# Where split weights lie in on-chip memory: one fixed byte offset for all feature-major projections instead of a different one per call

## The chip, the cores and the metric

The kernel runs on one core of one Trainium2 chip. The metric is the device time of one launch in microseconds (us). Before the change the median of three runs is 2135.49 us (2133.76 to 2135.58). The profile shown below is of one further execution, which took 2132.74 us; from its first to its last instruction it spans 2131.0 us. The engines are named as in the profile: PE is the matrix engine (its instruction that streams the moving operand), PEld its weight load, ACT the scalar engine, DVE the vector engine, POOL the general engine, SP the queue that issues the DMAs.

## The reference

One layer of a hybrid encoder on 256 tokens of width 2048, all in float32:

```python
h = rms_norm(x, norm_mix_g)
x = x + hybrid_mixer(h, ...)          # w_in: 2048 -> 18464, retention + gated DeltaNet, w_out: 2048 -> 2048
h = rms_norm(x, norm_x_g);  mem_n = rms_norm(mem, norm_mem_g)
x = x + cross_attention(h, mem_n, w_xq, w_xkv, w_xo)      # 4 heads, 256 memory tokens
h = rms_norm(x, norm_ffn_g)
x = x + square(relu(h @ w_ff1)) @ w_ff2                   # 2048 -> 8192 -> 2048
return rms_norm(x, norm_final_g)
```

Nearly all of the arithmetic is dense projections of 256 tokens through weights that are read from the chip's main memory once.

## The kernel before, in words

**Products in two parts.** Each float32 operand is kept as two float32r operands, a high part and a low part, with value = high + low. A product takes three of the four partial products: high x high, high x low, low x high. The activations lie as `q` tiles: 128 partitions by 4 feature blocks by 512 columns, of which the first 256 are the high parts of the 256 tokens and the other 256 the low parts (`quad.both` is all 512).

**Fetching weights.** `fetch` (lines 75 to 97) brings one piece of 1 MB into a tile `raw` (one of three buffers), with one DMA on the SP queue. It then makes two halves of 1024 columns each: ACT copies the half into a tile `whi` (line 94, which rounds to float32r), DVE subtracts that from `raw` into a tile `wlo` (line 95). `whi` and `wlo` have three buffers each. Each buffer is 1024 + 64 floats long per partition, 4352 bytes, and the 1024 floats that are used start `a` floats into it; the argument `at` gives `a` for `whi` and for `wlo`.

**Two kinds of projection.** Both go through `fetch`.

- `chunk` (lines 122 to 152) is token-major: the stationary operand is 128 tokens of `q`, the moving operand is 512 columns of `whi` or `wlo` (lines 135 to 137). It takes four fetches a call and uses the default `at=(0, 0)`.
- `blocks` (lines 159 to 187) is feature-major: the stationary operand is a block of 128 x 128 from `whi` or `wlo`, the moving operand is `q`. For each block and each of the 16 feature blocks it issues a pair: line 177 multiplies the block of `whi` with all 512 columns of `q`, line 178 the block of `wlo` with the 256 high columns. A call with `nb=2` has 16 x 2 = 32 pairs, takes two fetches (four halves of 8 pairs), and gives 256 output features. At its end ACT and DVE add the two halves of the PSUM tile (lines 182 and 183) and hand the result on.

**The placement in `blocks`.** A counter `turn` counts the calls of `blocks` in the order of the program. Call n, counted from 0, takes `ah, al = divmod(29 * n % 64, 8)`, and `at=(8 * ah, 8 * al)` floats: the used part of `whi` starts 32 * ah bytes, that of `wlo` 32 * al bytes into its buffer, with ah and al from 0 to 7. As 29 is odd, 64 calls in a row go through all 64 pairs (ah, al), and call n + 64 has the pair of call n again. Such a pair is called a placement below.

**The order of the calls of `blocks`**, 97 in all:

| calls | what | when, us |
|---|---|---|
| 0 | decay inputs, `nb=1`, 16 pairs | 86 |
| 1 to 8 | keys of the cross-attention | 114 to 212 |
| 9 to 40 | q, k, v of the DeltaNet (6 a group) and q, k of the retention (2 a group), four groups | 212 to 992 |
| 41 to 48 | `w_out` | 1117 to 1208 |
| 49 to 56 | queries of the cross-attention | 1208 to 1316 |
| 57 to 64 | `w_xo` | 1317 to 1412 |
| 65 to 96 | first MLP matrix, four groups of 8 | 1412 to 2035 |

In the MLP each group of 8 calls of `blocks` is followed by 4 calls of `chunk`.

**The order of the work.** The order of the instructions on each engine is made by a planner when the program is built, from the dependences and from priorities. DMAs and the two steps of a split have the highest priority (line 79), evacuations the next (line 180). Nothing is ordered by hand around the change.

**Where the tiles lie.** Along each partition lie first the three buffers of `raw`, then the three of `whi`, then the three of `wlo`, then the `q` tiles and all else. Two small unused tiles (`PAD1`, 32 bytes, line 280, and `PAD2`, 320 bytes, line 814) shift the later `q` tiles. With `at=(0, 0)` the used parts of `whi` and `wlo` and all `q` tiles start at the same remainder to 256 bytes; this is the common offset.

Of the kernel before, what the change touches and what calls it, by code (L numbers as in the profile page):

```python
# [3 lines left out]

# [8 lines left out]
F32R = mybir.dt.float32r  # L13
# [5 lines left out]
P = 128  # L19
# [11 lines left out]
C_GA, C_GZ, C_TA, C_TB = 12288, 12320, 14368, 16416  # L31
THETA = 10000.0

PAD1, PAD2 = 8, 80
TWO_PI = 2.0 * math.pi
BIG = 1.0e30
# [14 lines left out]
def trunk(ctx: ExitStack, tc: tile.TileContext, x, mem, positions, norm_mix_g, w_in, conv_w, gdn_a_log, gdn_dt_bias,  # L51
# [8 lines left out]
    wp = ctx.enter_context(tc.tile_pool(name="wpipe", bufs=3))  # L60
# [5 lines left out]
    def stream_ps():  # L66
        s0 = psp.tile([P, 512], F32, name="s0", tag="s0", bufs=2)
        s1 = psp.tile([P, 512], F32, name="s1", tag="s1", bufs=2)
        return s0, s1
# [5 lines left out]
    def fetch(pieces, k, n, rush=False, hold=None, at=(0, 0)):  # L75


        raw = wp.tile([P, k * n], F32, name="raw", tag="raw", bufs=3)
        rv = raw.rearrange("p (k n) -> p k n", k=k)
        with tc.high_priority(offset=100000):  # L80
            for off, ap in pieces:
                src = ap.rearrange("(k p) n -> p k n", p=P)
                for ks in ((slice(0, k // 2), slice(k // 2, k)) if rush else (slice(0, k),)):
                    nc.sync.dma_start(rv[:, ks, off:off + ap.shape[1]], src[:, ks, :])
            got = []
            for i in range(2):
                if hold:
                    both = hold().both
                    hi, lo = (both[:, a:a + 2, :].rearrange("p a s -> p (a s)") for a in (0, 2))
                else:  # L90
                    hi, lo = (wp.tile([P, k * n // 2 + 64], F32R, name=nm, tag=nm, bufs=3)[:, a:a + k * n // 2]
                              for nm, a in zip(("whi", "wlo"), at))
                src = raw[:, i * k * n // 2:(i + 1) * k * n // 2]
                act.activation(hi, src, AF.Copy)  # L94
                vec.tensor_sub(lo, src, hi.bitcast(F32))  # L95
                got.append((hi.rearrange("p (k n) -> p k n", n=n), lo.rearrange("p (k n) -> p k n", n=n)))
        return got
# [23 lines left out]
    def chunk(quads, pieces_of, evac, before=None, hold=None):  # L121
# [4 lines left out]
        if hold:  # L126
            parts[1:] = [(1, 0, 256, ps[1][:, :256]), (1, 256, 512, bank()[:, :256])]
        held = {q: fetch(pieces_of(q), 4, 512, hold=hold) for q in ((2, 3) if hold else ())}

        def products(q, i, part, halves):  # L130
# [8 lines left out]
        for q in range(4):  # L139
            if q not in held:  # L140
                if before:
                    before(q)
                halves = fetch(pieces_of(q), 4, 512, rush=before is not None and q == 0)
                for i in range(4):
                    for part in parts:
                        products(q, i, part, halves)
# [7 lines left out]
    def cols(w, c0, n=512):  # L154
        return lambda q: [(0, w[q * 512:(q + 1) * 512, c0:c0 + n])]

    turn = itertools.count()

    def blocks(quads, w, c0, nb, evac):

        k = 16 // nb

        ah, al = divmod(next(turn) * 29 % 64, 8)
        ps = stream_ps()
        n = nb * P
        for g in range(KT // k):
            halves = fetch([(0, w[g * k * P:(g + 1) * k * P, c0:c0 + n])], k, n, at=(8 * ah, 8 * al))
            for i in range(k):  # L170
                kk = g * k + i
                xh, xhl = quads[kk // 4][0][:, kk % 4, :], quads[kk // 4].both[:, kk % 4, :]
                wh, wl = halves[i // (k // 2)]
                for b in range(nb):
                    bs = slice(b * P, (b + 1) * P)
                    lh, ll = wh[:, i % (k // 2), bs], wl[:, i % (k // 2), bs]
                    pe.matmul(ps[b], lh, xhl, start=kk == 0, stop=False)  # L177
                    pe.matmul(ps[b][:, :S], ll, xh, start=False, stop=kk == KT - 1)  # L178
        for b in range(nb):
            with tc.high_priority(offset=50000):  # L180
                o = sm.tile([P, S], F32, name="bo", tag="bo", bufs=2)
                act.activation(o, ps[b][:, S:], AF.Copy)  # L182
                vec.tensor_add(o, o, ps[b][:, :S])  # L183
                evac(b, o)
# [131 lines left out]
    for k2 in range(8):  # L316
# [10 lines left out]
        for f in range(2):  # L327
            k = 2 * k2 + f
# [160 lines left out]

    values(2)  # L490
    blocks(h1, w_in[0], C_GA, 1, decay_rows)
    values(3)
    for h in range(4):
# [6 lines left out]
    for b2 in range(8):  # L500
        ko = kv.tile([P, 2, S], F32, name="ko", tag="vo", bufs=2)

        def evac_k(b, ps):
            vec.tensor_mul(ko[:, b, :], ps, mrow)

        blocks(memq, w_xkv[0], b2 * 256, 2, evac_k)
        nc.sync.dma_start(kt_d[:, 2 * b2:2 * b2 + 2, :], ko)
        if b2 < 4:
            for h in (2 * b2, 2 * b2 + 1):
                decays(8 + h)  # L510
                ret_decays(h)
# [17 lines left out]
    def gdn_stream(grp):  # L529
# [5 lines left out]
        for pr in range(2):  # L535
# [5 lines left out]
            for part, c0, bofs in ((1, C_GQ, 0), (0, C_GK, 16), (2, C_GV, 32)):  # L541
                def evac(b, ps, part=part, bofs=bofs):
                    if part < 2:
                        conv_silu(bofs + h0 + b, ps, kq[:, b, part, :])
                    else:
                        vt = mx.tile([P, S], F32, name="vt", tag="vt", bufs=2)
                        conv_silu(bofs + h0 + b, ps, vt)
                        vts.append(vt)
                blocks(h1, w_in[0], c0 + h0 * GD, 2, evac)
# [317 lines left out]
    for h in range(XH):  # L867
# [32 lines left out]
        for d2 in range(2):  # L900
            ops = bank()
            ov = ops.rearrange("p (d s) -> p d s", d=2)
            for d in range(2):
                c0 = (2 * d2 + d) * P
# [115 lines left out]
```

## Time and profile before

| | |
|---|---|
| median of three runs | 2135.49 us |
| the profiled execution | 2132.74 us |
| its span | 2131.0 us |
| PE busy | 2098.4 us (98%) |
| PEld busy | 1800.7 us (84%) |
| DVE busy | 1410.8 us (66%) |
| ACT busy | 1091.9 us (51%) |
| pairs of lines 177 and 178 | 3088 |
| matmuls of each of lines 135, 136, 137 on fetched weights | 1264 |

The time of a launch is the span and a few microseconds around it. PE records overlap: a matmul's record lasts until its modelled end, and the next one starts before that. So how fast PE goes is read from start to start, or from the length of a stretch in which nothing else runs on PE and the number of its matmuls, not from the mean duration of a record. In the answers by windows, the first two numbers are the ends of a stretch, then its length, then the busy time of PE in it with the number of instructions that touch the stretch, then the granted clock of PE as a share of the full one, the busy share of the DMA engines and the GB/s moved. A stretch that holds one call of 32 pairs shows 65 or 66 instructions, since the one or two before it overlap its start. A stretch over eight such calls shows 513.

### The profile page before, as it was taken

Reading aid. Unit: us, or ns where it says so; the run is one execution under the profiler, and the core shown is the slowest. Engines: PE = TensorE matmul, PEld = TensorE weight load, DVE = VectorE, ACT = ScalarE, POOL = GpSimd, SP = SyncE. Lnnn points to the kernel's source line nnn. Section 1 sums busy time; section 2 is a strip of 40 time slices with the busy share of each in tenths; the row PEclk is TensorE's granted clock in tenths of the full one; section 3 lists DMA queues with packets and bytes.
Section 4 is the critical chain, followed back from the end, with each engine's and each line's share of the span. In section 5 each row is a group of like instructions: output and inputs, shape, how many; then the busy total and the mean of one; then the engine's idle time right before and its main releaser. Section 6 shows DMA issues by size and latency. Waiting matters only on the chain.

```text
span 2131.0 us, 28778 instructions
## 1 busy us (share of the span) xinstructions
PE 2098.4 (98%) x11172; PEld 1800.7 (84%) x11172; DVE 1410.8 (66%) x2225; ACT 1091.9 (51%) x1700; POOL 29.7 (1%) x39
## 2 busy tenths in 40 slices
PE   8999999799999999999999999999999999999998
PEld 6878888688898889888888889888888888888887
DVE  5766779588667866786557666766556555655655
ACT  7565565354556455645455555554434434434444
POOL 0000000000000000000000000000000000000000
PEclk9999999999999999999999999999999999999999
DMA  8777655356545654555458664566566556656653
GB/s 294 247 244 243 200 187 192 97 190 198 168 154 188 201 184 143 175 196 197 155 168 261 192 188 151 176 198 186 191 197 186 189 197 187 189 198 188 188 197 139
DMA packets 316009, 405.91 MB, mean 190 GB/s; under 512 B 16592, under 2 KB 224480, under 8 KB 315744
## 3 DMA queue, kind: packets, MB, share of 16 engines
q1 hardware_dynamic: 315872, 404.08, 58.8%
q8 instruction: 87, 1.43, 0.3%
q14 instruction: 50, 0.41, 0.1%
HBM read 390.40 MB, written 13.65 MB: 190 GB/s over the span
## 4 chain that ended last, share of the span: by engine, by line
PE 92%; DMA 3%; ACT 2%; DVE 1%; SPq 1%; issue 0%; POOL 0%; ACTq 0%; POOLq 0%; DVEq 0%
PE s L177 32%; PE s L178 16%; PE s L136 13%; PE s L135 13%; PE s L137 13%; PE b L656 2%; DMA row<-crow 1%; DMA dec_d<-dec_w 1%; DVE wlo L95 1%; ACT whi L94 1%; DMA xc<-x 1%; ACT dec_w L481 0%; PE b L567 0%; DMA ct<-scr_t 0%; PE b L105 0%
## 5 line engine op out<-in xcount | busy, mean ns | idle before, releaser
L95 DVE TENSOR_TENSOR wlo<-raw,whi 128x1024 fp32r<-128x1024 f32 x702 | 858.3, 1224 | 518.1 <-ACT whi L94 512.2
L94 ACT ACTIVATE whi<-raw 128x1024 fp32r<-128x1024 f32 x702 | 742.7, 1059 | 725.4 <-PE s L137 374.4
L177 PE MATMUL s<-q,whi 128*128 128x512 f32 x3088 | 1076.4, 395 | 1.3 <-DVE bo L183 0.9
L178 PE MATMUL s<-q,wlo 128*128 128x256 f32 x3088 | 846.6, 282 | 5.3 <-DVE wlo L95 5.2
L177 PEld LDWEIGHTS s<-q,whi 128*128 128x128 f32 x3088 | 572.3, 188 | 121.2 <-DVE bo L183 1.1
L178 PEld LDWEIGHTS s<-q,wlo 128*128 128x128 f32 x3088 | 580.8, 188 | 20.5 <-DVE wlo L95 9.0
L136 PE MATMUL s<-wlo,q 128*128 128x512 f32 x1264 | 494.1, 391 | 0.8 <-DVE wlo L95 0.8
L137 PE MATMUL s<-whi,q 128*128 128x512 f32 x1264 | 491.5, 390 | 0.0
L135 PE MATMUL s<-whi,q 128*128 128x512 f32 x1264 | 449.6, 391 | 0.0
L136 PEld LDWEIGHTS s<-wlo,q 128*128 128x128 f32 x1264 | 237.9, 188 | 50.1 <-DVE wlo L95 2.4
L135 PEld LDWEIGHTS s<-whi,q 128*128 128x128 f32 x1264 | 237.3, 188 | 49.9 <-ACT whi L94 0.5
L137 PEld LDWEIGHTS s<-whi,q 128*128 128x128 f32 x1264 | 237.6, 188 | 48.4
L182 ACT ACTIVATE bo<-s 128x256 f32<-128x256 f32 x193 | 72.8, 377 | 127.5 <-PE s L178 115.1
L183 DVE TENSOR_TENSOR bo<-bo,s 128x256 f32<-128x256 f32 x193 | 80.3, 416 | 49.1 <-ACT bo L182 48.9
L522 DVE SCALAR_TENSOR_TENSOR acc<-bo,cw,acc 128x255 f32<-128x255 f32 (+2 forms) x144 | 66.1, 478 | 2.0 <-ACT acc L519 1.0
L622 DVE TENSOR_TENSOR pr<-lw,tw 32x31 f32<-32x31 f32 (+15 forms) x124 | 40.4, 326 | 9.7 <-DMA lw<-scr_l 7.6
L624 DVE TENSOR_TENSOR tw<-tw,pr 32x31 f32<-32x31 f32 (+15 forms) x124 | 40.6, 328 | 2.6
L948 DVE SCALAR_TENSOR_TENSOR res<-s,rstd3q,res 128x512 f32<-128x512 f32 (+1 forms) x32 | 22.3, 736 | 11.8 <-PE s L137 11.8
L757 ACT ACTIVATE gth<-s 128x512 f32<-128x512 f32 x32 | 18.9, 590 | 18.5 <-PE s L137 15.5
L937 DVE SCALAR_TENSOR_TENSOR hs<-bo 128x256 f32<-128x256 f32 x64 | 27.0, 422 | 1.1
L940 DVE TENSOR_TENSOR q<-hs,q 128x256 fp32r<-128x256 f32 x64 | 26.8, 419 | 0.9 <-ACT q L939 0.9
L939 ACT ACTIVATE q<-hs 128x256 fp32r<-128x256 f32 x64 | 26.2, 410 | 0.0
(292 smaller groups left out, 1083.7 us busy)
## 6 DMA issues: line engine op xcount, KB each, us to landing
raw<-w_in SPq DMA_DIRECT2D x144, 1024.0 KB, 5.1
raw<-w_ff SPq DMA_DIRECT2D x128, 1024.0 KB, 5.4
raw<-w_xkv SPq DMA_DIRECT2D x31, 1024.0 KB, 6.3
raw<-w_out SPq DMA_DIRECT2D x16, 1024.0 KB, 5.6
raw<-w_xq SPq DMA_DIRECT2D x16, 1024.0 KB, 6.6
raw<-w_xo SPq DMA_DIRECT2D x16, 1024.0 KB, 5.4
dec_d<-dec_w SPq DMA_DIRECT2D x16, 192.0 KB, 4.9
dec<-dec_d SPq DMA_DIRECT2D x8, 384.0 KB, 3.2
```

The source lines that it names most:

```text
L94: act.activation(hi, src, AF.Copy)
L95: vec.tensor_sub(lo, src, hi.bitcast(F32))
L135: pe.matmul(o, xh, wh, start=first, stop=False)
L136: pe.matmul(o, xh, wl, start=False, stop=False)
L137: pe.matmul(o, xl, wh, start=False, stop=last)
L177: pe.matmul(ps[b], lh, xhl, start=kk == 0, stop=False)
L178: pe.matmul(ps[b][:, :S], ll, xh, start=False, stop=kk == KT - 1)
L182: act.activation(o, ps[b][:, S:], AF.Copy)
L183: vec.tensor_add(o, o, ps[b][:, :S])
L522: vec.scalar_tensor_tensor(acc[:, d:], ps[:, :S - d], cw[:, j, blk:blk + 1], acc[:, d:], op0=ALU.mult, op1=ALU.add)
L624: vec.tensor_sub(tw[:, j + 1:32, 0:j + 1], tw[:, j + 1:32, 0:j + 1], pv)
L656: pe.matmul(pv[:, i, :], lhs(i), rhs[:, i, :], start=True, stop=True)
```

## The change

All calls of `blocks` take one placement: `whi` starts 56 floats (224 bytes) into its buffer, `wlo` 0 floats. That is the pair (7, 0) of the pairs above, which calls 24 and 88 have before. The counter is gone. The buffers of `wlo` lose their room of 64 floats and are now 4096 bytes long instead of 4352; those of `whi` keep it. So the second and third buffer of `wlo` start 256 and 512 bytes earlier and all that lies behind them 768 bytes earlier. `chunk` keeps `at=(0, 0)`.

```diff
-import itertools
 ...
+AT_BLOCKS = (56, 0)
 ...
-                    hi, lo = (wp.tile([P, k * n // 2 + 64], F32R, name=nm, tag=nm, bufs=3)[:, a:a + k * n // 2]
-                              for nm, a in zip(("whi", "wlo"), at))
+                    hi, lo = (wp.tile([P, k * n // 2 + room], F32R, name=nm, tag=nm, bufs=3)[:, a:a + k * n // 2]
+                              for nm, a, room in zip(("whi", "wlo"), at, (64, 0)))
 ...
-    turn = itertools.count()
-
     def blocks(quads, w, c0, nb, evac):
         k = 16 // nb
-
-        ah, al = divmod(next(turn) * 29 % 64, 8)
         ps = stream_ps()
         n = nb * P
         for g in range(KT // k):
-            halves = fetch([(0, w[g * k * P:(g + 1) * k * P, c0:c0 + n])], k, n, at=(8 * ah, 8 * al))
+            halves = fetch([(0, w[g * k * P:(g + 1) * k * P, c0:c0 + n])], k, n, at=AT_BLOCKS)
```

## The prediction

> **What bounds the kernel now.** I read the page of the profile first: the busy shares, then the chain of work that ended last, then the costliest groups.
>
> ```profile
> span 2131.0 us, 28778 instructions
> PE 2098.4 (98%) x11172; PEld 1800.7 (84%) x11172; DVE 1410.8 (66%) x2225; ACT 1091.9 (51%) x1700; POOL 29.7 (1%) x39
> ...
> PE 92%; DMA 3%; ACT 2%; DVE 1%; SPq 1%; issue 0%; POOL 0%; ACTq 0%; POOLq 0%; DVEq 0%
> ...
> L177 PE MATMUL s<-q,whi 128*128 128x512 f32 x3088 | 1076.4, 395 | 1.3 <-DVE bo L183 0.9
> L178 PE MATMUL s<-q,wlo 128*128 128x256 f32 x3088 | 846.6, 282 | 5.3 <-DVE wlo L95 5.2
> ```
>
> PE is busy for 2098.4 of 2131.0 us and carries 92% of the chain that sets the end. The two lines that the change touches wait almost never (1.3 and 5.3 us in 3088 pairs). So the pace of a pair goes into the time one for one, wherever the pair itself is not starved. The pace is not in the means of 395 and 282 ns, since the records overlap. It is in the starts, read from the timeline of PE in call 88:
>
> ```profile
> 1850.11 0.39 PE L177 MATMUL s<-q,whi 128*128 128x512 f32 x1
> 1850.34 0.28 PE L178 MATMUL s<-q,wlo 128*128 128x256 f32 x1
> 1850.45 0.39 PE L177 MATMUL s<-q,whi 128*128 128x512 f32 x1
> ```
>
> From one line 177 to the next it is 0.34 us. For a finer number, stretches of whole calls serve, read by windows on PE alone. First the calls 73 to 80, 81 to 88 and 89 to 96 (eight each, 256 pairs), and two stretches of `chunk` between them:
>
> ```profile
> 1592.87:1682.43 89.56, 89.56 (x513) 1.00 0.61 188
> 1769.51:1858.74 89.23, 89.23 (x513) 1.00 0.62 189
> 1945.80:2035.20 89.39, 89.39 (x513) 1.00 0.62 189
> 1505.82:1592.87 87.05, 87.05 (x386) 1.00 0.59 193
> 1682.43:1769.51 87.08, 87.08 (x386) 1.00 0.58 193
> ```
>
> PE has no gap in them and its clock is the full one. The mean call takes (89.56 + 89.23 + 89.39) / 24 = 11.174 us, or 349.2 ns a pair. The two stretches of `chunk`, 384 matmuls each on an unvaried placement, agree to 0.03 us. Calls of `blocks` do not agree with each other; here are the eight of the middle group, in order, and with them their placements (ah, al): (5,5), (1,2), (4,7), (0,4), (4,1), (7,6), (3,3), (7,0).
>
> ```profile
> 1769.51:1780.71 11.20, 11.20 (x65) 1.00 0.63 187
> 1780.71:1791.86 11.15, 11.15 (x66) 1.00 0.63 190
> 1791.86:1802.95 11.10, 11.10 (x66) 1.00 0.62 189
> 1802.95:1814.06 11.10, 11.10 (x66) 1.00 0.62 190
> 1814.06:1825.32 11.26, 11.26 (x66) 1.00 0.63 186
> 1825.32:1836.58 11.26, 11.26 (x66) 1.00 0.64 188
> 1836.58:1847.70 11.12, 11.12 (x66) 1.00 0.60 189
> 1847.70:1858.74 11.04, 11.04 (x66) 1.00 0.57 192
> ```
>
> The same instructions on the same shapes take 11.04 to 11.26 us, with PE never idle. Is it the placement? Each placement comes again 64 calls later, so the trace holds its own repeat. First calls 9, 10, 11 and 20, with (0,5), (4,2), (7,7) and (0,4), then calls 73, 74 and 75, which repeat the first three (call 84, above, repeats the fourth):
>
> ```profile
> 212.35:223.51 11.16, 11.16 (x66) 1.00 0.80 265
> 223.51:234.64 11.12, 11.12 (x66) 1.00 0.66 209
> 234.64:245.76 11.13, 11.13 (x66) 1.00 0.58 189
> 367.51:378.63 11.12, 11.12 (x66) 1.00 0.59 189
> ...
> 1592.87:1604.11 11.24, 11.24 (x65) 1.00 0.63 187
> 1604.11:1615.24 11.12, 11.12 (x66) 1.00 0.64 190
> 1615.24:1626.36 11.12, 11.12 (x66) 1.00 0.63 189
> ```
>
> Three of the four come back within 0.02 us over a thousand microseconds later, in another stage, with another `q`; (0,5) misses by 0.08. So most of the spread belongs to the placement. The placement that the change gives to all calls, (7,0), stands before in calls 88 (11.04, above) and 24:
>
> ```profile
> 535.05:546.14 11.09, 11.09 (x66) 1.00 0.55 191
> ```
>
> Both are at or under the shortest of the others quoted (11.10).
>
> **The change part by part.** (a) The pace. The two visits of (7,0) give (11.04 + 11.09) / 2 = 11.065 us, 0.109 us under the mean call of 11.174. There are 96 calls of 32 pairs and one of 16, so 96.5 calls: 96.5 x 0.109 = 10.5 us less PE work. The two ends are the two visits: at 11.09 it is 96.5 x 0.084 = 8.1 us, at 11.04 96.5 x 0.134 = 12.9 us. I take the middle: (7,0) is the lowest of many, and the lowest of many visits flatters itself, so I don't go to the better end.
>
> (b) Where the gain is not passed on. Before about 205 us the keys of the cross-attention share the time with decay tables, and PE is held up there:
>
> ```profile
> 115.00:205.00 90.00, 85.44 (x478) 71.70 (x477) 52.61 (x82) 58.05 (x142) 0.00 (x0) 1.00 0.81 257
> ...
> DVE em L477 <- DMA row<-crow: 15.8, 12, 3.1
> ACT dec_w L481 <- DMA dec_d<-dec_w: 8.6, 5, 3.9
> ```
>
> The first row is a window over all engines (PE, PEld, DVE, ACT, POOL in order), the other two are of the waits in the same window. 478 instructions are some 7.5 calls; at 11.174 us they would fill 84 us of the 90. What waits here is DVE and ACT on DMAs of the decay tables, and both feed PE. Whatever PE saves in these 7.5 calls it may lose again at the next late split: 7.5 x 0.109 = 0.8 us. I take all of it off, since shorter PE work does not bring a DMA forward. Elsewhere, lines 177 and 178 are not kept waiting, and I take nothing off. Sum: 10.5 - 0.8 = 9.7 us, with ends 7.3 and 12.1.
>
> (c) The splits. ACT writes `whi` at another start, DVE writes `wlo` at another. Over all 64 placements and the unshifted calls of `chunk` their times are as good as constant (min/median/max in ns):
>
> ```profile
> L94 ACT ACTIVATE whi<-raw x702: 1040/1061/1092, 4.9 to 2103.5; 128x1024 fp32r<-128x1024 f32 x176
> L95 DVE TENSOR_TENSOR wlo<-raw,whi x702: 1149/1225/1228, 6.0 to 2104.8; 128x1024 fp32r<-128x1024 f32 x176
> ```
>
> The bounds are 1092 - 1061 = 31 ns a split worse and 76 ns better, on 386 splits each in `blocks` 12 us more ACT or 29 us less DVE work; DVE has 34% of the span free and ACT 49%, and PE hides it. I take nothing. If that cover were gone, 12 us on the chain would turn the sign.
>
> (d) `chunk`, and everything moved by the shorter `wlo`. The buffers of `wlo` step by 4096 bytes and not 4352, and what lies behind moves by 768; all of these shifts are multiples of 256. Before, the three buffers already differ from each other by an odd multiple of 256 (4352 is 17 x 256), and every call of `blocks` goes through all of them while the rows above still repeat. `chunk` keeps its pace over three buffers (87.05 against 87.08). So I take nothing for the shifts. The bounds come from the spread of the `blocks` rows: if a longer remainder counted, a call could come out anywhere from 11.04 to 11.26, and the `chunk` stretches could move by the 0.03 us seen between them.
>
> No instruction, DMA, wait or queue is added, removed or reordered by the text of the change. So the profiled execution should take 2132.74 - 9.7 = 2123.0 us. The median of the runs stands 2135.49 - 2132.74 = 2.75 us over it, so I forecast 2125.8.
>
> **A rule that speaks against it.** The rows say that a pair's pace hangs on where the stationary operand lies. The Trainium skill says otherwise. In "TensorE: Matmul & The Clock Gate", section "Step-by-step: what each phase is for", the streaming operand and the weight load have two independent read ports, and loading the next weights doesn't take read bandwidth from the running matmul; in "SBUF — State Buffer", section "SBUF: two separate sides", it says that on the engines' side "only the shared port pair causes contention" and that TensorE never waits on anyone. By that, all placements are worth the same and the sum is 0, which is the first rival below. The repeats (11.12 and 11.12, 11.13 and 11.12, 11.12 and 11.10, against 11.26) disagree with it, though they do not show which reads collide.
>
> **The rivals.** *Nothing happens.* The rows differ for a reason that only looks like the placement, for example what ran just before, and a program with one placement throughout settles at the mean of 11.174: 2135.5. For it: (0,5) took 11.16 and then 11.24. Against it: the other repeats.
>
> *The feeding engines take it back.* PE's gain turns into waits for the splits where DVE is busiest, in calls 9 to 40 beside the DeltaNet work: 32 x 0.109 = 3.5 us lost, which leaves 6.2 us of gain: 2129.3. For it: line 178 already waits 5.2 us on line 95. Against: 5.2 us is all there is in 2131, and 0.109 us a call is little beside it.
>
> *The slow rhythm.* A run of matmuls can settle into more than one rhythm at one placement: (0,5) differs by 0.08 us from visit to visit. If (7,0) throughout, with other distances to `q` or with itself as the neighbour, falls into a rhythm like that of the two slowest rows (11.26), each call loses 11.26 - 11.174 = 0.086 us, in all 96.5 x 0.086 = 8.3: 2143.8. It is slower than before once over 0.109 / (0.109 + 0.086) = 56% of the pairs run so. For it: nothing in the two visits. Against: both are below the mean, in two stages with different `q` tiles.
>
> **How the numbers follow.** I give the forecast 0.79, nothing happens 0.11, the feeding engines 0.04, the slow rhythm 0.06. A change of 0.2%, 4.3 us, is about what a measurement of this kernel can tell from none. The forecast and the feeding engines are faster by more than that, so faster 0.83, within 0.11, slower 0.06. The range: the ends of the sum are 2135.5 - 12.1 = 2123.4 and 2135.5 - 7.3 = 2128.2. The runs before spread over 1.8 us, and a rhythm of the last bound throughout with nothing lost at the start would be another 0.8 lower, so I go down to 2121.0. Upwards I go to 2131.5, past the feeding engines; it leaves out the other two rivals, 0.17.
>
> **What would show it right or wrong.** In the changed trace, all calls of `blocks` in the MLP should take 11.04 to 11.09 us, and a group of eight 88.3 to 88.7 against 89.2 to 89.6; the spread between calls should be gone; the `chunk` stretches should stay at 87.1; the splits at 1061 and 1225 ns; the waits of line 178 about 5 us. The forecast is wrong if the groups of eight stay at 89.4 (nothing happens), if they shorten but the span does not (the feeding engines; then lines 177 and 178 show idle time), if they reach 90 (the slow rhythm), or if the `chunk` stretches move (a longer remainder counts).

## The result and the profile after

The changed kernel takes 2123.86 us in the median of six runs (2121.83 to 2126.97), beside 2135.53 us before (2133.76 to 2140.12, six runs). The ratio is 0.9944, with a 95% interval from 0.9931 to 0.9957: faster, by 0.43% to 0.69%. The profiled execution took 2124.05 us, with a span of 2122.3 us. The forecast was 2125.8 us.

In the changed file the lines have moved: the pair of `blocks` is now at lines 174 and 175, the splits at 95 and 96, `chunk` at 136 to 138. First the page of the changed kernel's profile:

```profile
span 2122.3 us, 28778 instructions
PE 2088.8 (98%) x11172; PEld 1800.5 (85%) x11172; DVE 1409.7 (66%) x2225; ACT 1091.6 (51%) x1700; POOL 29.7 (1%) x39
...
L174 PE MATMUL s<-q,whi 128*128 128x512 f32 x3088 | 1067.4, 392 | 1.2 <-DVE bo L180 0.9
L175 PE MATMUL s<-q,wlo 128*128 128x256 f32 x3088 | 847.3, 282 | 6.6 <-DVE wlo L96 6.6
```

PE's busy time fell by 9.6 us and the span by 8.7; the other engines did the same work as before. Line 174, whose records fell from 395 to 392 ns in the mean, carries the difference; line 175 hardly changed. Its waits for the late split are 6.6 us, 1.4 more than before.

Now PE by windows in the changed kernel: the three groups of eight calls in the MLP (calls 73 to 80, 81 to 88, 89 to 96), the four calls of `chunk` between the first two, then call 88 alone.

```profile
1587.46:1675.75 88.29, 88.29 (x513) 1.00 0.62 191
1762.83:1851.12 88.29, 88.29 (x513) 1.00 0.62 191
1938.19:2026.48 88.29, 88.29 (x513) 1.00 0.61 191
1675.75:1762.83 87.08, 87.08 (x386) 1.00 0.58 193
1840.09:1851.12 11.03, 11.03 (x66) 1.00 0.58 192
```

The spread between calls is gone. Each group takes 88.29 us, where the three took 89.56, 89.23 and 89.39 before; the call is 11.03 us, 344.8 ns a pair. `chunk` is where it was.

Where along the span did the time go? The next rows are windows on PE from call 17 to call 23, on to call 41, and to the end. First the kernel before, then the changed one; the window from call 6 to call 17 stands last in each:

```profile
331.89:523.01 191.12, 180.27 (x947) 0.99 0.50 164
523.01:1117.03 594.02, 593.19 (x3128) 1.00 0.53 176
1117.03:2131.03 1014.00, 1005.83 (x5425) 1.00 0.60 189
178.62:331.89 153.27, 153.27 (x858) 1.00 0.64 205
```

```profile
331.15:523.27 192.12, 181.29 (x948) 0.98 0.50 163
523.27:1116.13 592.86, 592.09 (x3127) 1.00 0.54 176
1116.13:2122.33 1006.20, 998.01 (x5425) 1.00 0.60 191
179.40:331.15 151.75, 151.75 (x859) 1.00 0.65 207
```

The last 56 calls of `blocks` gain 1014.00 - 1006.20 = 7.80 us, 0.139 us a call. Up to call 17 the gain is 0.74 us (331.89 - 331.15), calls 23 to 40 gain 1.16, and the stage between them loses 1.00. So nine tenths of the profile's gain comes from the second half of the span.

### The profile page after: what moved, and what is told of

It reads as the page before. It is cut to its first block, busy times and chain, and to the rows that moved or that the text cites. A ratio compares the mean times of both kernels' runs of the same rounds, so it can differ in the third digit from the quotient of the medians.

```text
span 2122.3 us, 28778 instructions
## 1 busy us (share of the span) xinstructions
PE 2088.8 (98%) x11172; PEld 1800.5 (85%) x11172; DVE 1409.7 (66%) x2225; ACT 1091.6 (51%) x1700; POOL 29.7 (1%) x39
## 4 chain that ended last, share of the span: by engine, by line
PE 93%; DMA 3%; DVE 1%; ACT 1%; SPq 1%; issue 0%; POOL 0%; ACTq 0%; POOLq 0%; DVEq 0%
PE s L174 32%; PE s L175 16%; PE s L137 13%; PE s L138 13%; PE s L136 13%; PE b L653 2%; DMA row<-crow 1%; DMA xc<-x 1%; DMA dec_d<-dec_w 1%; DVE wlo L96 1%; PE b L564 0%; PE b L106 0%; DMA ct<-scr_t 0%; PE b L108 0%; PE b L107 0%
```

## The experiments

My theory: the distance between the weights and `q`, as its remainder to 256 bytes, sets how fast a pair goes, and (224, 0) is a fast one. The rivals were that the shorter buffers of `wlo` do it, that it is the sameness of the placement from call to call, and that the trace of before had misled me.

### Full room for `wlo`, a longer `whi` offset, and a slow placement

```diff
 # e1_room
-                              for nm, a, room in zip(("whi", "wlo"), at, (64, 0)))
+                              for nm, a, room in zip(("whi", "wlo"), at, (64, 64)))
 # e4_256
-AT_BLOCKS = (56, 0)
+AT_BLOCKS = (120, 0)          # room (128, 0)
 # e2_slow
-AT_BLOCKS = (56, 0)
+AT_BLOCKS = (40, 48)          # room (64, 64)
```

> The changed kernel, with the 64 floats of room given back to the buffers of wlo: the one placement (224, 0) stays, and everything lies where it lay before the change. If the placement alone makes the gain, a call of 32 pairs takes 11.03 us in the MLP as in the changed kernel and the median is some 2124 us, 0.994 of the kernel before. If the shorter buffers of wlo (other distances to q and to each other) have a part in it, the calls fall back towards the 11.17 us of before, and the median towards 2135.

> The changed kernel with whi 256 bytes further, 480 bytes from the common offset (room of 512 bytes in its buffers). If only the remainder to 256 bytes counts, a call of the MLP takes 11.03 us as in the changed kernel. If a longer remainder counts, it takes another time, anywhere from 11.03 to 11.28 us.

> The kernel before with one placement for all calls, but with a slow one: whi 160 bytes and wlo 192 bytes from the common offset, the pair (5, 6), which took 11.26 us in call 70 before. If the placement sets the pace, every call of the MLP takes 11.26 us, 0.09 above the mean call of before, and 96.5 calls make it some 8 us slower: 2144, 1.004 of the kernel before. If it is the sameness of the placement from call to call that brings the gain, whichever it is, the calls come down to 11.03 and the median to 2124.

Measured, the middle group of the MLP by windows on PE, in e1_room, e4_256 and e2_slow:

```profile
1770.81:1859.10 88.29, 88.29 (x513) 1.00 0.63 191
```

```profile
1763.21:1851.50 88.29, 88.29 (x513) 1.00 0.62 191
```

```profile
1783.13:1873.51 90.38, 90.38 (x513) 1.00 0.61 187
```

The room makes no difference, nor do 256 bytes more. The slow placement takes 90.38 / 8 = 11.30 us a call (11.26 expected), the same in every group, and the whole is slower than before: ratio 1.0043, from 1.0026 to 1.0060, a median of 2145.07 us in five runs against 2136.82 (a sixth run, of 5511.55 us, is not in these numbers). e4_256 had one run only, of 2124.42 us. So the sameness of the placement isn't the cause: one placement throughout can be worse than the rotation. e1_room's median is 2130.05 us, ratio 0.9956 (0.9937 to 0.9976), more than the changed kernel's 2123.86 though its calls take the same time; the second profile of before suggests why.

### The kernel before, profiled again

No edit.

> The kernel before, unchanged, profiled a second time, for the stage up to 1117 us, in which the changed kernel's profile gains 0.9 us only, where 40.5 calls at 0.11 to 0.14 us would give 4.4 to 5.7. If the first profile of before had a fortunate start, this one is some 3 us later at call 41 (1120 us) and the same as the first from there on. If the gain is lost there to waits, it is at 1117 us again.

It took 2144.06 us, 11.3 more than the first profile, and was 11.3 us later at call 41, where some 3 had been expected. A window from 390 to 435 us and the same four windows as above, then the window from 390 to 435 us in the first profile and in e1_room:

```profile
390.00:435.00 45.00, 33.18 (x159) 0.70 0.14 43
332.36:533.32 200.96, 189.14 (x948) 0.93 0.50 156
533.32:1128.31 594.99, 593.64 (x3128) 1.00 0.56 176
1128.31:2142.33 1014.02, 1005.84 (x5425) 1.00 0.60 189
179.10:332.36 153.26, 153.26 (x859) 1.00 0.65 205
```

```profile
390.00:435.00 45.00, 34.15 (x213) 0.96 0.20 65
```

```profile
390.00:435.00 45.00, 33.86 (x171) 0.73 0.11 38
```

From call 41 on, the two profiles of the same kernel agree to 0.02 us (1014.00 and 1014.02), and the groups do to 0.01. All that sets them apart lies ahead of it, and 9.8 of the 11.3 us between call 17 and call 23. There the first group's DeltaNet recurrence leaves PE waiting in short gaps, and the granted clock falls: to 0.96 of full in the mean in one execution, to 0.70 in another. In the second profile it is 0.50 throughout from 404 to 418 us. It happens to the changed kernels too (0.92 in the changed kernel, 0.73 in e1_room). So two executions of the same kernel differ by 9.8 us between call 17 and call 23, more than the 8.7 us by which the change shortened the profile. The stage's loss of 1.00 us in the profile after, and e1_room's median, are probably of this kind: three runs of e1_room with a mean clock of 0.993 or 0.994 took 2132.01 to 2133.56 us, the three with 0.996 to 0.998 2124.48 to 2128.09. So from here on kernels are compared by the groups of the MLP, where the clock is 1.00. By the Trainium skill ("TensorE: Matmul & The Clock Gate", section "HAM oscillation — how this bites in real kernels"), gaps of PE above some 3.4 us let the clock fall to half. In the first group's recurrence most of PE's gaps are 0.7 to 0.8 us with 1.2 us of work between, and the longest from 390 to 435 us is 1.44 us, as two rows of the timeline of the kernel before show (the gap ahead of a row is in brackets); in the second profile the longest is 2.18 us.

```profile
395.59 1.16 PE L656 MATMUL b<-w,am 128*128 128x128 f32 x8 [0.69 <-ACT w L668]
417.92 0.38 PE L569 MATMUL b<-kh 128*128 128x256 f32 x1 [1.44 <-DVE yg L690]
```

So the clock fell here where the gaps are shorter than that; what decides between 0.96 and 0.70 is open.

### Is it the distance to `q`?

```diff
 # e3_qshift: 32 bytes ahead of the q tiles
+    hqp.tile([P, 8], F32, name="padq")
 # e10_allshift: 32 bytes ahead of raw, whi, wlo, q and all else
+    wp.tile([P, 8], F32, name="padw", bufs=1)
```

> The changed kernel with 32 bytes of padding ahead of the q tiles, so that all q tiles and all that lies behind them start 32 bytes later, while whi and wlo stay. If the distance between the weights and q decides, the pair (7, 0) turns into (6, 7), whose call 35 had 348.8 ns a pair before: a call of the MLP takes 11.16 us. If the place of the weights alone decides (the remainder of their own addresses), it stays at 11.03.

> The changed kernel with 32 bytes of padding ahead of raw, so that raw, whi, wlo, q and all that lies behind them start 32 bytes later, their distances unchanged. If the pace hangs on the distances between the weights and q, the groups of eight take 88.29 us as in the changed kernel, where moving q alone took them to 89.33. If the own address of q or of the weights counts, they take another time, 89.33 or whatever else.

The middle group, then the four calls of `chunk` behind it, in e3_qshift and in e10_allshift:

```profile
1791.04:1880.37 89.33, 89.33 (x513) 1.00 0.62 189
1880.37:1969.96 89.59, 89.59 (x386) 1.00 0.57 188
```

```profile
1769.92:1858.21 88.29, 88.29 (x513) 1.00 0.63 191
1858.21:1945.29 87.08, 87.08 (x386) 1.00 0.58 193
```

With `q` 32 bytes further, a call takes 89.33 / 8 = 11.17 us, as the trace of before said for the distances that this makes (11.16). With everything 32 bytes further it is 11.03 again. So, for these shifts, it is the distances that count, not the addresses. And `chunk`, whose distances the change leaves alone, answers too: 89.59 against 87.08 us, 2.9%, with `q` now 32 bytes off its weights. Both kernels had single runs only (2158.69 and 2131.16 us).

### Maps: finer steps in `blocks`, the rotation in `chunk`

```diff
 # e5_map, room (64, 64): call n of blocks
-            halves = fetch([...], k, n, at=AT_BLOCKS)
+            halves = fetch([...], k, n, at=(4 * (turn % 16), 4 * (turn // 16 % 4)))
 # e6_chunkmap, room (64, 64): call n of chunk; blocks keeps AT_BLOCKS
+        ch, cl = divmod(next(turns) * 29 % 64, 8)
 ...
-                halves = fetch(pieces_of(q), 4, 512, rush=before is not None and q == 0)
+                halves = fetch(pieces_of(q), 4, 512, rush=before is not None and q == 0, at=(8 * ch, 8 * cl))
```

> A map in finer steps: call n of blocks lays whi 16 * (n mod 16) bytes and wlo 16 * (n / 16 mod 4) bytes from the common offset. If the pace depends on the address by units of 32 bytes, a placement at an odd multiple of 16 takes the time of the multiple of 32 below it (within 0.05 us a call); if it is finer, odd multiples come out otherwise, and some may go under the 11.03 us of (224, 0). If 11.03 is the floor of these matmuls, none goes under it by more than 0.02.

> The changed kernel with the rotation of before given to chunk instead: its call n lays whi 32 * ah and wlo 32 * al bytes from the common offset with ah, al = divmod(29 n mod 64, 8), and blocks keeps (224, 0). Before and after, with (0, 0), four calls of chunk take 87.07 us in the MLP, 226.8 ns a matmul. If only weights that are the stationary operand feel their place, chunk stays at 21.77 us a call. If any distance between stationary and moving operand counts, its calls spread as those of blocks did, by up to 2%: 21.77 to 22.2 us; and if (0, 0) is not its best, some go below 21.7.

e5_map, calls 84 at (64, 16) bytes, 68 at (64, 0) and 85 at (80, 16):

```profile
1808.68:1819.67 10.99, 10.99 (x66) 1.00 0.64 192
1455.87:1466.90 11.03, 11.03 (x67) 1.00 0.63 192
1819.67:1830.79 11.12, 11.12 (x66) 1.00 0.64 189
```

(64, 16) and (80, 16), which lie 16 bytes apart in `whi`, differ by 0.13 us, and the first is below the 11.03 us that I had taken for the floor. Call 79 at (240, 0), right behind call 78 at (224, 0), takes 11.17 us against its 11.06. So steps of 16 bytes probably count; but these are single calls, whose pace also depends on what ran ahead (next section), and no kernel with an odd multiple of 16 bytes for `whi` throughout was run. The second row was a surprise: (64, 0) is the pair (2, 0), which took 11.19 us in call 80 of before, and here 11.03 (the row of call 80 follows). The same placement at the same distances had two times.

```profile
1671.24:1682.43 11.19, 11.19 (x66) 1.00 0.57 189
```

e6_chunkmap, the first two groups of `blocks`, and the `chunk` stretch behind the first (the third group takes 90.32 us again, the second stretch of `chunk` 89.03):

```profile
1599.56:1687.83 88.28, 88.28 (x513) 1.00 0.63 191
1776.97:1867.29 90.32, 90.32 (x513) 1.00 0.61 187
1687.83:1776.97 89.14, 89.14 (x386) 1.00 0.57 189
```

`chunk` lost 2 us of 87 wherever its placement rotated, so its (0, 0) had been better than the mean of the rotation, and by more than (224, 0) is for `blocks`. Its calls there take 22.1 to 22.4 us; 21.77 to 22.2 had been expected. And `blocks`, with nothing changed in it, took 90.32 us in two of the three groups. Here are the starts of two pairs of each rhythm by the timeline of PE, four pairs apart, first of e6_chunkmap in its second group, then of the changed kernel:

```profile
1789.65 0.40 PE L178 MATMUL s<-q,whi 128*128 128x512 f32 x1
...
1791.06 0.40 PE L178 MATMUL s<-q,whi 128*128 128x512 f32 x1
```

```profile
1775.61 0.39 PE L174 MATMUL s<-q,whi 128*128 128x512 f32 x1
...
1776.99 0.39 PE L174 MATMUL s<-q,whi 128*128 128x512 f32 x1
```

Four pairs take 1.41 us in the one and 1.38 in the other, at the same placement, and so for eight calls on end. The groups of matmuls in the second group say where: line 178 of e6_chunkmap, then line 174 of the changed kernel.

```profile
L178 PE MATMUL s<-q,whi 128*128 128x512 f32 x256 | 89.7, 398 | 0.0
```

```profile
L174 PE MATMUL s<-q,whi 128*128 128x512 f32 x256 | 87.6, 389 | 0.0
```

The 512-column matmul takes all of it: its records are 9 ns longer. From its start to that of the next matmul it is 235 or 236 ns in the slow rhythm nearly every time, mostly 224 to 229 in the fast one; from the 256-column one it is 116 to 119 in both. e5_map and e6_chunkmap had one run each (2138.62 and 2145.58 us).

### Does the entry choose the rhythm?

```diff
 # e8_entry, room (64, 64): three calls of chunk alone
+        lay = {27: (8, 56), 31: (0, 24), 35: (48, 56)}.get(next(turns), (0, 0))
 ...
+                halves = fetch(pieces_of(q), 4, 512, rush=before is not None and q == 0, at=lay)
```

> The changed kernel with full room for wlo and with other placements in three calls of chunk alone, each of them the last one ahead of a group of eight calls of blocks in the MLP: call 27 of chunk takes (1, 7), 31 takes (0, 3), 35 takes (6, 7), all others (0, 0). These are the calls that stood there in the map of chunk, after which blocks at (224, 0) took 88.28, 90.32 and 90.32 us a group. If the rhythm of a group is set by how it is entered, the groups take 88.3, 90.3 and 90.3 us again. If it was something else in that kernel (its other chunk calls, or the distances with full room), all three take 88.29.

The three groups in e8_entry:

```profile
1590.52:1678.79 88.28, 88.28 (x513) 1.00 0.62 191
1766.36:1856.68 90.32, 90.32 (x513) 1.00 0.61 187
1944.29:2034.61 90.32, 90.32 (x513) 1.00 0.61 187
```

They came out as in the map (one run, 2132.15 us). One call of `chunk` ahead of a group, laid otherwise, costs the group behind it 2.03 us against the changed kernel's 88.29, though the group itself is the same. So one placement has more than one rhythm, and what ran ahead decides which of them the group falls into and then keeps; how it decides stays open. It also limits what single runs say of a placement. The groups of e2_slow stand behind `chunk` calls that lie as in the changed kernel, so there the placement alone makes the difference; in e3_qshift the distances of `chunk` moved as well, and its 89.33 us are neither of the two rhythms seen at (224, 0).

### A faster placement

```diff
-AT_BLOCKS = (56, 0)           # room (64, 0)
+AT_BLOCKS = (16, 4)           # room (64, 64)
```

> The changed kernel with the placement that was the fastest in the map in finer steps: whi 64 bytes, wlo 16 bytes from the common offset (full room for wlo). There its call 84 took 10.994 us, its call 20 11.058. If a call keeps to the better of these, a group of eight takes 87.95 us, 0.34 less than the changed kernel, and the whole is 96.5 * 0.039 = 3.8 us faster than that: 2120. If that call was a favourable entry, the group takes 88.5 (11.06 a call) or more, and the median is 2126 or above.

> The changed kernel, unchanged, beside the one with (64, 16), on the same chip. Its groups of eight take 88.29 us, its median 2122 to 2130, depending on how long the clock is halved between 390 and 435 us.

The middle group with (64, 16):

```profile
1761.02:1849.03 88.01, 88.01 (x513) 1.00 0.63 192
```

88.01 us, 11.00 a call, so the call of the map had not been a favourable entry; calls alternate between 10.995 and 11.01 us. In call 84 the first 16 pairs take 5.45 us and the other 16 take 5.54, so even here only half a call runs at the faster pace. Against the same runs of the kernel before (median 2142.95 us), it takes 2122.10 us (2118.44 to 2124.86), ratio 0.9905 (0.9886 to 0.9924), and the changed kernel 2127.45 us (2125.17 to 2132.38), ratio 0.9939 (0.9916 to 0.9961); the changed kernel's groups are 88.29 us again. All four runs of the new placement lie under all four of the changed kernel. The intervals of the ratios overlap, so by how much it is faster stays open; in the profiles it is 0.28 us a group where the clock is full.

## Why the prediction was right

**The pace, (a).** Right in kind: the trace of before held the time of this placement, and the placement sets it (e2_slow, e3_qshift, e10_allshift). The size was taken too low: 0.109 us a call from the mean of the two visits, where 0.139 was measured over the last 56 calls. The better visit, 11.04, was the true one: in the groups of the MLP every call takes the 11.03 us of call 88. The visit of 11.09 was not chance either, since call 24 takes 11.08 in the changed kernel: the two visits differ by where in the program they stand. On these 56 calls the term missed 56 x 0.030 = 1.7 us. The repeats that the forecast rested on were a kind choice. Of the ten calls from 6 to 20 that have nothing else between their pairs, nor have when their placement comes again, five come back within 0.03 us, three differ by 0.04 to 0.08, and calls 18 and 19 by 0.11 to 0.12.

**Where it is not passed on, (b).** Half of this step failed. I took the gain off for the first 7.5 calls and took nothing off elsewhere. The first half held as far as can be seen: call 6 starts at 178.62 us in the kernel before and at 179.40 in the changed one (179.10 and 179.02 in their second profiles), so no gain shows ahead of it. Behind it calls 6 to 16 gain 153.27 - 151.75 = 1.52 us, 0.138 a call, as the last stage does. What failed is that elsewhere the gain is passed on whole. Calls 25 to 30 and 33 to 38, with the DeltaNet's matmuls between their pairs, show it: first before, then changed.

```profile
569.32:654.27 84.95, 84.95 (x539) 1.00 0.48 157
792.51:877.75 85.25, 85.25 (x539) 1.00 0.48 156
```

```profile
569.53:654.42 84.88, 84.88 (x539) 1.00 0.48 157
792.32:877.20 84.88, 84.88 (x539) 1.00 0.49 157
```

These 12 calls gain 0.07 + 0.37 = 0.44 us, where the step has 12 x 0.109 = 1.3; the second profiles of both kernels give the same lengths to 0.01 us. PE is never idle in them, so the gain isn't lost to a wait, which is where I had looked for a loss. It is lost to the rhythm. Here are starts of line 174 in the changed kernel from call 35 into call 36, ten pairs apart before and ten pairs apart behind matmuls of the DeltaNet (line 653):

```profile
823.40 0.39 PE L174 MATMUL s<-q,whi 128*128 128x512 f32 x1
...
826.85 0.39 PE L174 MATMUL s<-q,whi 128*128 128x512 f32 x1
...
832.26 1.05 PE L653 MATMUL b<-w,am 128*128 128x128 f32 x8
...
833.50 0.40 PE L174 MATMUL s<-q,whi 128*128 128x512 f32 x1
...
837.03 0.40 PE L174 MATMUL s<-q,whi 128*128 128x512 f32 x1
```

Ten pairs take 3.45 us in the one stretch and 3.53 in the other, at one placement. Between the two stretches stand eight more matmuls of line 653 (at 827.08) and ten pairs in 3.46 us, a third pace. By the starts, some 90 of the 384 pairs of these 12 calls go at the slow pace, 8 ns a pair over the fast one, and some 80 at the third, 2 ns over it: 0.9 us, which is what is missing. So the rhythm changes at the other matmuls between the pairs, as it does behind one call of `chunk` in e8_entry. No run takes those matmuls away.

**The sum.** By stages, in us, the terms of the forecast beside the two profiles:

| calls | forecast | measured |
|---|---|---|
| 0 to 16 | 16.5 x 0.109 - 0.8 = 1.0 | 0.74 |
| 17 to 22 | 6 x 0.109 = 0.65 | -1.00 |
| 23 to 40 | 18 x 0.109 = 1.96 | 1.16 |
| 41 to 96 | 56 x 0.109 = 6.1 | 7.80 |
| all | 9.7 | 8.70 |

That the totals are so near is in part luck: what (a) took too low in the last stage makes up for most of what (b) and the stage with the fallen clock, which no term held, took away. The second profiles of the two kernels put calls 23 to 40 at 594.99 and 593.18 us, so the 1.16 itself varies by half a microsecond or more. For the median I carried over the 2.75 us by which it stood over the profiled execution before; after the change it stands 0.19 us under it. So the medians moved by 11.67 us, the profiled executions by 8.69. The clock is the likely reason, as the first profile of before had it at 0.96 from 390 to 435 us where the second had 0.70, but no run tells its part in the medians.

**The splits and the shifts, (c) and (d).** As said: the splits stay at 1061 and 1225 ns in the median, `chunk` at 87.08 us, and e1_room and e4_256 show that multiples of 256 bytes count for nothing. What (d) didn't see is that `chunk` is as sensitive (2.9% in e3_qshift); the change leaves its distances alone.

**The rivals.** *Nothing happens* fell with the groups. *The feeding engines* fell too: the waits of the pair grew from 6.6 to 7.8 us only. *The slow rhythm* is real. At (224, 0) it takes 90.32 / 8 = 11.29 us a call, as e6_chunkmap and e8_entry show, which is slower than the mean before; with all of 96.5 calls in it, 96.5 x (11.29 - 11.174) = 11.2 us would have been lost. The changed kernel runs in it in parts of calls 25 to 38, as shown above, and in the whole of call 50:

```profile
1216.98:1228.27 11.29, 11.29 (x66) 1.00 0.59 186
```

I gave it 0.06 and argued against it from two visits. Two visits can't tell that a placement has no second rhythm; that the groups of the MLP fell into the fast one was luck as far as the forecast goes.

**The rule of the Trainium skill** ("TensorE: Matmul & The Clock Gate", section "Step-by-step: what each phase is for") that the weight load and the streaming operand have independent read ports and take nothing from each other would make all placements worth the same. Here it doesn't hold to the last 2.7%: behind the same `chunk` calls, the same 256 pairs take 88.01 to 90.38 us by where their operands lie, with PE never idle. Which reads collide, if it is the reads, isn't shown by these runs.

## What to carry to other kernels

When PE is the bound and every call does the same work, read single calls of the trace against each other, not the mean: a spread that comes back with the address is worth having, and a kernel that varies its placement from call to call has tried all of them in one run, each behind one neighbour. Try a placement in the whole kernel before trusting it, since its pace also depends on what runs ahead of it, and compare by stages in which the clock is full. Where an event of the clock is as large as the change, two profiles of the same kernel tell more than one profile of each.

## What the runs showed of the hardware that I had not expected

- A stream of equal matmuls has more than one lasting pace at one placement (11.03 and 11.29 us a call with `whi` at 224 and `wlo` at 0 bytes), and what ran ahead of the stream chooses; eight calls on end keep it. Eight matmuls of another kind in between are enough to change it (ten pairs in 3.45, 3.46 or 3.53 us).
- Steps of 16 bytes probably matter: 10.99 us a call at (64, 16), 11.12 at (80, 16), by single calls.
- Where the weights are the moving operand, the distance to `q` is worth up to 2.9% as well (87.08 against 89.59 us a stretch).
- The granted clock falls in a stage where PE is busy for three quarters of the time in short pieces, in some executions for much longer than in others (0.96 and 0.70 of full over the same 45 us of the same program).
